# A decoder layer in split fp32 on one Trainium2 core: low weight parts of 30 column tiles through an adding DMA

## The chip, the cores and the metric

The kernel runs on one core of one Trainium2 chip. The metric is the device time of one execution in microseconds (us), the median of several runs.

## The reference: what is computed

One step of a hybrid decoder layer for a prompt of 512 tokens and 8 single sample tokens, width 1024, all in fp32. A normalised input goes through one combined projection `w_in` of 5632 columns. They feed three branches: A, a gated linear recurrence with a short convolution; B, a GLU with a causal depthwise convolution of 31 taps; C, a diagonal state space model with a GLU of its own. Three gates of 1024 columns each weigh the branches' projections; then come an output projection and a feed-forward block.

```
proj = rms_norm(x, g_mix) @ w_in
u_a, z_b, u_c, gate_in = split(proj)
y_a = rg_lru(causal_dwconv(u_a))
y_b = silu(layer_norm(causal_dwconv(z_b[:512] * sigmoid(z_b[512:]))))
y_c = glu(gelu(s5_ssm(u_c)))
g_a, g_b, g_c = sigmoid(gate_in + b_gate)
x = x + (g_a * (y_a @ w_pa) + g_b * (y_b @ w_pb) + g_c * (y_c @ w_pc)) @ w_out
x = x + (silu(h2 @ w1) * (h2 @ w2)) @ w_ffn_out        where h2 = rms_norm(x, g_ffn)
```

## The kernel before

Activations lie transposed, channels on the 128 partitions and the 520 tokens along the free axis, in two halves of 260. A weight matrix is worked on in column tiles of 128 columns; for `w_in` each has 8 tiles of 128 rows.

**Split products.** TensorE takes its operands in a rounded form (type fp32r), so that each fp32 operand is split into a rounded high part and the rest, the low part. `prod` (L243 to 251) does for each column tile high times high, high times the activations' low part, and then low weights times high activations: 48 matmuls of 260 columns in two halves, the 32 with the high weights ahead of the 16 with the low ones.

**Weights.** `wload` (L214) loads a pair of column tiles (1 MB) into `wraw`, by a DMA on the queue of SyncE (SP); there are two such buffers, so that a load waits until both columns of the pair before the last have been read. `wsplit` (L222) makes the parts of one column: ScalarE writes the high part `whi` (L225), and DVE or GpSimd (POOL), whichever `eng` names, subtracts it from the raw column and writes the low part `wlo` (L226). `whi` and `wlo` have three buffers each, so the parts of column n go where those of column n-3 lay. `wcol` (L231) calls both, with high priority.

```
whi, wlo: bufs=3        wraw: bufs=2
S.activation(hi, raw, AF.Copy)
e.tensor_tensor(lo, raw, hi.bitcast(F32), op=ALU.subtract)
```

The keys of `w_in`'s column tiles are `w.in.0` to `w.in.43`: branch A's 0 to 7, B's 8 to 15, C's 16 to 19, and the gates 20 to 43.

**Order.** PE's order of work is written out by hand (the string `ORDER`). The instructions of the other engines are put in an order when the kernel is built, by a scheduler with priorities; each engine and each DMA queue then works in that order. SP's queue carries, beside the raw weights, the loads `h<-ud_d` for branch C (`c_prep`, L870), the gate weights `w_rg` and `w_ig` of branch A (`a_load`, L1082), and the stores of finished gates, `g_d<-t` (`gate`, L1296). On DVE the 116 instructions of the 31 taps (`b_conv`, L1231) have low priority and fill in. An activation is split by ScalarE (L257) and DVE or GpSimd (L258).

**Names at the places of the prediction.** On GpSimd `pend_s` (L932), the copy of `s_rho` (L817), `fin_a` (L1134, L1135) and L938 to L941 are small steps of the states of branches A and C. `t L257` is the high part of a product of a gate or of branch A.

Of the kernel before, what the change touches and what calls it, by code (L numbers as in the profile page):

```python
# [16 lines left out]
F32 = mybir.dt.float32  # L17
F32R = mybir.dt.float32r
I32 = mybir.dt.int32
AF = mybir.ActivationFunctionType  # L20
ALU = mybir.AluOpType
# [10 lines left out]
ON_POOL = set("""  # L32
ac.3 caz.2 caz.3 ebz.0 ebz.1 ebz.2 ebz.3 hs.0 hs.2 hs.4 hs.5 rho.1 rho.2 rho.3 w.glu.3 w.in.0 w.in.10 w.in.11 w.in.2
w.in.3 w.in.36 w.in.38 w.in.39 w.in.4 w.in.8 w.w_out.3 w.w_pa.2 w.w_pa.5 w.w_pa.6 w.w_pb.1 w.w_pb.4 w.w_pb.5 w.w_pc.2
w.w_pc.3 wrg.6 ya.5 yg.0 yg.2
""".split())

ON_DVE = set("""
ca.0 ca.1 ca.2 ca.3 wt.0 wt.1 wt.2 wt.3
""".split())  # L40
# [15 lines left out]
def hybrid_step(ctx: ExitStack, tc, a, o):  # L56
    nc = tc.nc
    V, S, G, T, Y = nc.vector, nc.scalar, nc.gpsimd, nc.tensor, nc.sync
# [10 lines left out]

    def eng(key):  # L70

        return G if key in ON_POOL else V

    uid = [0]

    def nm(s):
        uid[0] += 1
        return f"{s}_{uid[0]}"
# [4 lines left out]
    def ht(shape, dt=F32):  # L83
        return hp.tile(shape, dt, tag="h", name=nm("h"))
# [70 lines left out]
    def vload(names, eng):  # L155
        nonlocal at
        for name in names:
            src = a[name][0]
            src = (src.rearrange("k (t p) -> (k t) p", p=P) if name.startswith("w_conv") else
                   src.rearrange("(t p) -> t p", p=P))  # L160
            VB[name] = at
            eng.dma_start(vrow[at:at + src.shape[0], 1, :], src)
            at += src.shape[0]
# [58 lines left out]
    def wsplit(raw, nk, e, dst=None):  # L222
        hi, lo = dst or (wp.tile([P, nk, P], F32R, tag="whi", name=nm("whi"), bufs=3),
                         wp.tile([P, nk, P], F32R, tag="wlo", name=nm("wlo"), bufs=3))
        S.activation(hi, raw, AF.Copy)  # L225
        e.tensor_tensor(lo, raw, hi.bitcast(F32), op=ALU.subtract)  # L226
        return hi, lo

    pend = {}
# [1 line left out]
    def wcol(src, key, c, nk, k0=0, pair=True, dst=None):  # L231

        with tc.high_priority():
            e = eng(f"w.{key}.{c}")
            if not pair:
                return wsplit(wload(src, c * P, nk, P, k0), nk, e, dst)
            if (key, c) not in pend:
                raw = wload(src, c * P, nk, 2 * P, k0)
                pend[(key, c)] = raw[:, :, 0:P]
                pend[(key, c + 1)] = raw[:, :, P:2 * P]  # L240
            return wsplit(pend.pop((key, c)), nk, e)
# [203 lines left out]
    for k in range(8):  # L445
# [8 lines left out]
                           op=ALU.mult))  # L454
# [307 lines left out]
    def c_pool(ct):  # L762

        d = st_c.setdefault(ct, {})
        E = eng(f"eb.{ct}")
        s_ = slice(4 * ct, 4 * ct + 4)
        eb = d["eb"] = ht([P, 2, 4, P])
# [28 lines left out]

        E = V if f"wt.{ct}" in ON_DVE else G
        wt = d["wt"] = ht([P, 2, 4, P])
# [21 lines left out]
    def c_pool2(ct):  # L820

        d = st_c[ct]
        s_ = slice(4 * ct, 4 * ct + 4)
        E = V if f"ca.{ct}" in ON_DVE else G
        ca = d["ca"] = ht([P, 2, 4, P])
# [534 lines left out]
    for c in range(8):  # L1360
        w = wcol(a["w_out"][0], "w_out", c, 8)
# [4 lines left out]
        hi, lo = fh[c // 4][:, c % 4, :], fl[c // 4][:, c % 4, :]  # L1366
# [135 lines left out]
    for half, (f0, f1) in enumerate(((0, 12), (12, 22))):  # L1502
        act = {}
        for f in range(f0, f1, 2):
# [9 lines left out]
            for j in range(2):  # L1514
                w = wcol(w_fi, "fi", f + j, 8)
# [11 lines left out]
            for j in range(2):  # L1527
                w = wcol(w_fi, "fi", NF + f + j, 8)
# [24 lines left out]
        for c in range(8 if half == 0 else 4):  # L1553
            w = [wcol(w_fo, "fo", c, hk, k0=f0 + j * hk, pair=False) for j in range(2)]
# [11 lines left out]
    for h in range(2):  # L1566
        for c in range(4, 8):
            ps = mm()
            for j in range(2):
# [9 lines left out]
                hi, lo = wk[c, j]  # L1579
# [54 lines left out]
```

## Time and profile before

| | |
|---|---|
| median of 3 runs | 908.58 us (907.57 to 910.23) |
| the profiled execution | 913.02 us |
| its span in the trace | 910.4 us |
| mean granted clock of TensorE | 0.978 |
| PE busy | 859.9 us |
| DVE busy | 584.2 us |
| ScalarE (ACT) busy | 359.5 us |
| GpSimd (POOL) busy | 211.5 us |

The durations below come from the one profiled execution, which took 913.02 us; the span is the part of it that the trace covers. PE are the matmuls; the trace gives for each instruction its start, its duration and the idle time ahead of it with what ended that.

### The profile page before, as it was taken

What the parts mean: (1) busy time and instruction counts of PE and PEld (TensorE: products, weight loads), DVE (VectorE), ACT (ScalarE), POOL (GpSimd) and SP (SyncE); (2) the same over time, 40 slices, a digit from 0 to 9 for tenths busy, and PEclk for the clock granted to TensorE, in tenths of its full rate; (3) what the DMA queues carried; (4) which work ended last, traced back from release to release, by engine and by line L of the source; (5) the groups of instructions that cost most, each with busy time, mean ns of one, the idle gap of its engine ahead of it and who ended that gap; (6) DMA issues with size and microseconds to landing.
All of it is one profiled execution on the core that took longest, in us unless ns stands there. A gap on an engine that the chain in (4) does not pass through costs nothing.

```text
span 910.4 us, 17515 instructions
## 1 busy us (share of the span) xinstructions
PE 859.9 (94%) x7329; PEld 849.6 (93%) x7329; DVE 584.2 (64%) x977; ACT 359.5 (39%) x553; POOL 211.5 (23%) x294
## 2 busy tenths in 40 slices
PE   6989999879978499999999999999999999999997
PEld 5989999779878499999999999999999999999997
DVE  6799969777899999986674454444432344443443
ACT  5543243546467564516343433333211232233321
POOL 6467474426332602214111200000000000000021
PEclk9989999999998599999999999999999999999999
DMA  5833224232321126554262223332233432311322
GB/s 190 260 128 105 84 93 128 61 94 71 116 70 60 58 94 188 196 175 166 70 233 93 93 93 121 96 98 67 70 87 90 155 94 93 117 62 46 101 73 94
DMA packets 103630, 99.73 MB, mean 110 GB/s; under 512 B 8676, under 2 KB 94936, under 8 KB 103024
## 3 DMA queue, kind: packets, MB, share of 16 engines
q1 hardware_dynamic: 103215, 98.01, 33.8%
q8 instruction: 57, 0.93, 0.4%
q0 software_dynamic: 320, 0.57, 0.2%
q14 instruction: 22, 0.17, 0.1%
q10 hardware_dynamic: 16, 0.03, 0.0%
HBM read 86.57 MB, written 12.58 MB: 109 GB/s over the span
## 4 chain that ended last, share of the span: by engine, by line
PE 75%; DVE 12%; DMA 3%; POOL 3%; ACT 3%; issue 2%; SPq 1%; DVEq 0%; POOLq 0%; ACTq 0%
PE mm L251 69%; PE mm L1583 3%; DVE t L1231 3%; DMA t<-w_ig 1%; DVE wlo L226 1%; DVE q L1231 1%; SPq L198 1%; DMA wraw<-w_in 1%; ACT t L137 1%; DMA q<-x_prompt 1%; DMA g_d<-t 1%; POOL t L938 1%; POOL fin_a L1134 1%; DVE t L418 1%; ACT whi L225 0%
## 5 line engine op out<-in xcount | busy, mean ns | idle before, releaser
L251 PE MATMUL mm<-q,whi 128*128 128x260 f32 x3296 | 418.8, 284 | 1.4 <-ACT q L257 0.6
L251 PEld LDWEIGHTS mm<-q,whi 128*128 128x128 f32 x3296 | 405.4, 189 | 3.2 <-ACT t L137 1.0
L226 DVE TENSOR_TENSOR wlo<-wraw,whi 128x1024 fp32r<-128x1024 f32 (+3 forms) x126 | 140.2, 1113 | 219.3 <-PE mm L251 122.6
L225 ACT ACTIVATE whi<-wraw 128x1024 fp32r<-128x1024 f32 (+3 forms) x146 | 139.1, 956 | 239.3 <-PE mm L251 220.2
L251 PE MATMUL mm<-q,wlo 128*128 128x260 f32 x1648 | 215.4, 282 | 0.0
L251 PEld LDWEIGHTS mm<-q,wlo 128*128 128x128 f32 x1648 | 204.5, 188 | 0.0
L251 PE MATMUL mm<-h,whi 128*128 128x260 f32 x800 | 106.4, 287 | 2.9 <-DVE h L258 2.9
L251 PEld LDWEIGHTS mm<-h,whi 128*128 128x128 f32 x800 | 101.5, 192 | 3.5 <-DVE h L258 3.4
L1455 POOL TENSOR_TENSOR t<-t,t 128x260 f32<-128x260 f32 (+1 forms) x9 | 8.4, 931 | 370.9 <-DVE h L1430 336.5
L226 POOL TENSOR_TENSOR wlo<-wraw,whi 128x1024 fp32r<-128x1024 f32 (+1 forms) x20 | 43.4, 2168 | 76.1 <-PE mm L251 53.4
L251 PE MATMUL mm<-h,wlo 128*128 128x260 f32 x400 | 56.2, 286 | 0.0
L1231 DVE SCALAR_TENSOR_TENSOR t<-q,vec,t 128x512 f32<-128x512 f32 x71 | 53.3, 778 | 0.0
L251 PEld LDWEIGHTS mm<-h,wlo 128*128 128x128 f32 x400 | 52.2, 192 | 0.0
L137 ACT ACTIVATE t<-mm,vec 128x520 f32<-128x520 f32 x44 | 30.1, 693 | 37.9 <-PE mm L251 16.2
L137 ACT ACTIVATE t<-t,zero_t 128x520 f32<-128x520 f32 x30 | 21.5, 729 | 56.6 <-DVE t L1524 56.6
L251 PE MATMUL mm<-t,t 128*128 128x260 f32 x96 | 19.1, 361 | 23.9 <-ACT t L257 19.5
L251 PEld LDWEIGHTS mm<-t,t 128*128 128x128 f32 x96 | 16.7, 254 | 25.8 <-ACT t L257 20.4
L131 ACT ACT_TABLE_LOAD x22 | 28.2, 1283 | 1.1 <-PEq L1622 0.7
L257 ACT ACTIVATE h<-t 128x520 fp32r<-128x520 f32 x18 | 11.5, 637 | 42.7 <-DVE t L591 42.7
L1231 DVE SCALAR_TENSOR_TENSOR q<-q,vec 128x512 f32<-128x512 f32 x30 | 27.7, 923 | 0.4
L1120 POOL TENSOR_TENSOR t<-t,t 128x520 f32<-128x520 f32 x8 | 12.4, 1556 | 40.9 <-DVE t L1231 22.7
L591 DVE TENSOR_TENSOR t<-t,t 128x520 f32<-128x520 f32 x30 | 20.8, 700 | 0.7
(401 smaller groups left out, 913.1 us busy)
## 6 DMA issues: line engine op xcount, KB each, us to landing
wraw<-w_ffn_in SPq DMA_DIRECT2D x22, 1024.0 KB
wraw<-w_in SPq DMA_DIRECT2D x20, 1024.0 KB
g_d<-t SPq DMA_DIRECT2D x24, 260.0 KB
t<-g_d SPq DMA_DIRECT2D x24, 260.0 KB
wraw<-w_ffn_out SPq DMA_DIRECT2D x16, 384.0 KB
wraw<-w_ffn_out SPq DMA_DIRECT2D x16, 320.0 KB
wraw<-w_pa SPq DMA_DIRECT2D x4, 1024.0 KB
wraw<-w_out SPq DMA_DIRECT2D x4, 1024.0 KB
```

The costliest lines, as they stand in the source:

```text
L131: last_tab[0] = after(S.preload_act_table_set(SETS[func]), last_tab[0])
L137: last_tab[0] = after(S.activation(out, x, func, **kw), last_tab[0])
L198: Y.dma_start(craw[:, ri, hf, q * 64:(q + 1) * 64], a[n][0].rearrange("(h s q) c p -> h q s c p", h=2, q=2)[hf, q])
L225: S.activation(hi, raw, AF.Copy)
L226: e.tensor_tensor(lo, raw, hi.bitcast(F32), op=ALU.subtract)
L251: T.matmul(ps[:, h, 0:HN], w_, x[:, h * HN:(h + 1) * HN], start=first and i == 0, stop=last and i == n - 1)
L257: S.activation(hi, src, AF.Copy)
L418: seq("v", V.scalar_tensor_tensor(out, x, gmx[:, k:k + 1], r, op0=ALU.mult, op1=ALU.mult))
L591: V.tensor_tensor(out, x, y, op=ALU.mult)
L1120: G.tensor_tensor(ig, ig, c, op=ALU.mult)
L1231: ins = V.scalar_tensor_tensor(x, win(k), wdw(k, t), x, op0=ALU.mult, op1=ALU.add)
L1583: T.matmul(ps[:, 0, 0:HN], w[:, k, :], x[:, h * HN:(h + 1) * HN], start=j == 0 and k == 0 and i == 0, stop=j == 1 and k == hk - 1 and i == 2)
```

## The change

For 30 of the 44 column tiles of `w_in` (`ON_DMA`: branch A's, all of the gates but 36 and 37) the low part is made in another way. ScalarE writes the high part as before, then writes the negated rounded column into `wlo`, and a DMA on GpSimd's queue adds the raw column to what lies there. The source of that DMA is one half of the pair: 1,024 runs of 512 bytes. Without the change 24 of the 30 subtractions are DVE's and 6 GpSimd's.

```diff
--- before.py
+++ after.py
@@ -33,6 +33,12 @@
 ac.3 caz.2 caz.3 ebz.0 ebz.1 ebz.2 ebz.3 hs.0 hs.2 hs.4 hs.5 rho.1 rho.2 rho.3 w.glu.3 w.in.0 w.in.10 w.in.11 w.in.2
 w.in.3 w.in.36 w.in.38 w.in.39 w.in.4 w.in.8 w.w_out.3 w.w_pa.2 w.w_pa.5 w.w_pa.6 w.w_pb.1 w.w_pb.4 w.w_pb.5 w.w_pc.2
 w.w_pc.3 wrg.6 ya.5 yg.0 yg.2
+""".split())
+
+ON_DMA = set("""
+w.in.0 w.in.1 w.in.2 w.in.3 w.in.4 w.in.5 w.in.6 w.in.7 w.in.20 w.in.21
+w.in.22 w.in.23 w.in.24 w.in.25 w.in.26 w.in.27 w.in.28 w.in.29 w.in.30 w.in.31
+w.in.32 w.in.33 w.in.34 w.in.35 w.in.38 w.in.39 w.in.40 w.in.41 w.in.42 w.in.43
 """.split())
 
 ON_DVE = set("""
@@ -69,7 +75,7 @@
 
     def eng(key):
 
-        return G if key in ON_POOL else V
+        return None if key in ON_DMA else G if key in ON_POOL else V
 
     uid = [0]
 
@@ -223,7 +229,12 @@
         hi, lo = dst or (wp.tile([P, nk, P], F32R, tag="whi", name=nm("whi"), bufs=3),
                          wp.tile([P, nk, P], F32R, tag="wlo", name=nm("wlo"), bufs=3))
         S.activation(hi, raw, AF.Copy)
-        e.tensor_tensor(lo, raw, hi.bitcast(F32), op=ALU.subtract)
+        if e is None:
+
+            S.activation(lo, raw, AF.Copy, scale=-1.0)
+            G.dma_start(lo.bitcast(F32), raw, accum_op=ALU.add)
+        else:
+            e.tensor_tensor(lo, raw, hi.bitcast(F32), op=ALU.subtract)
         return hi, lo
 
     pend = {}
```

Line numbers behind `wsplit` are higher by 11 after the change. The scheduler also orders the engines anew; three places matter to the prediction.

**SP, the second load of a raw pair behind place A** (`wraw` a pair of columns, `h_2703` and `h_2713` the same tile of branch C, `t_2687` and `t_2697` the gate weights). Before:

```order
L218 DMA wraw_3183<-w_in 128x8x256
L870 DMA h_2703<-ud_d 32x4x136
L870 DMA h_2703<-ud_d 32x4x128 x2
L1082 DMA t_2687<-w_rg 128x2x128
L1082 DMA t_2687<-w_ig 128x2x128
```

After:

```order
L224 DMA wraw_3197<-w_in 128x8x256
L1093 DMA t_2697<-w_rg 128x2x128
L1093 DMA t_2697<-w_ig 128x2x128
L1307 DMA g_d<-t_2631 128x520
L881 DMA h_2713<-ud_d 32x4x136
L881 DMA h_2713<-ud_d 32x4x128
L1307 DMA g_d<-t_2688 128x520
```

The loads of `w_rg` and `w_ig` and a store of a gate have passed the loads from `ud_d`.

**GpSimd ahead of place A** (`wlo` rows are the adding DMAs; `wraw_2575` is the pair whose release lets the next load on SP start). Before:

```order
L932 COPY pend_s<-h_1827 128x4 x2
L881 MEMSET t_2269 128x96
L827 MEMSET h_2301 128x1024
L1071 COPY fin_a<-q_804 128x3
L1072 COPY fin_a<-q_804 128x8
```

After:

```order
L943 COPY pend_s<-h_1829 128x4 x2
L235 DMA wlo_2475<-wraw_2209 128x8x128
L892 MEMSET t_2276 128x96
L235 DMA wlo_2578<-wraw_2575 128x8x128
L838 MEMSET h_2308 128x1024
L235 DMA wlo_2635<-wraw_2575 128x8x128
L1082 COPY fin_a<-q_804 128x3
L1083 COPY fin_a<-q_804 128x8
```

Three adding DMAs stand between the same small steps.

**DVE at place D** (L1119 to L1133 before, L1130 to L1144 after: branch A's recurrence; L1231 and L1242: taps of the convolution, L1245 its last sum). Before:

```order
L591 TENSOR_TENSOR t_3439<-t_3439,t_2796 128x520
L1231 SCALAR_TENSOR_TENSOR t_3144<-q_801,vec,t_3144 128x2x256
L591 TENSOR_TENSOR t_3441<-t_3441,t_3142 128x520
L226 TENSOR_TENSOR wlo_3862<-wraw_3802,whi_3861 128x1024
L1231 SCALAR_TENSOR_TENSOR t_3149<-q_801,vec,t_3149 128x2x256
L1130 SCALAR_TENSOR_TENSOR q_803<-t_2787,t_3439 128x256
```

After:

```order
L1245 TENSOR_TENSOR t_3158<-t_3158,t_3163 128x2x256
L1138 TENSOR_TENSOR t_3481<-t_3147,h_806 128x8
L1130 SCALAR_TENSOR_TENSOR t_3457<-t_2797,t_3457 128x520
L1130 SCALAR_TENSOR_TENSOR t_3459<-t_3147,t_3459 128x520
L602 TENSOR_TENSOR t_3457<-t_3457,t_2806 128x520
L602 TENSOR_TENSOR t_3459<-t_3459,t_3156 128x520
L1141 SCALAR_TENSOR_TENSOR q_803<-t_2797,t_3457 128x256
L1139 TENSOR_TENSOR t_3481<-t_3481,t_3459 128x8
L1141 SCALAR_TENSOR_TENSOR q_803<-t_3147,t_3459 128x256
L1142 SCALAR_TENSOR_TENSOR q_803<-t_2797,q_803,t_3457 128x256
L1144 COPY q_803<-t_3481 128x2x4
L1142 SCALAR_TENSOR_TENSOR q_803<-t_3147,q_803,t_3459 128x256
```

The taps and the subtraction that stood between the recurrence's steps are gone from there; the taps stand ahead.

## Rows read from the trace of the kernel before

**Rows 1.** The page, busy time of each engine (share of the span) and instructions.
```profile
PE 859.9 (94%) x7329; PEld 849.6 (93%) x7329; DVE 584.2 (64%) x977; ACT 359.5 (39%) x553; POOL 211.5 (23%) x294
```

**Rows 2.** By stretch: busy us (count) of each engine, granted clock, DMA share, GB/s.
```profile
250.00:275.00 25.00, 19.33 (x156) 19.12 (x155) 25.00 (x39) 14.80 (x18) 7.62 (x6) 0.95 0.24 79
300.00:325.00 25.00, 16.79 (x94) 15.97 (x95) 25.00 (x33) 12.22 (x19) 14.32 (x12) 0.66 0.22 71
350.00:900.00 550.00, 549.11 (x4568) 547.83 (x4567) 278.57 (x366) 183.64 (x241) 45.00 (x34) 1.00 0.34 107
```

**Rows 3.** TensorE's waits: for what, us in total, times, longest us.
```profile
PE mm L251 <- ACT t L257: 19.5, 4, 9.1
```

**Rows 4.** Instructions on the raw weights: count, then ns min/median/max.
```profile
L226 DVE TENSOR_TENSOR wlo<-wraw,whi x126: 670/1222/2333, 30.4 to 878.7; 128x1024 fp32r<-128x1024 f32 x86, 128x768 fp32r<-128x768 f32 x16, 128x512 fp32r<-128x512 f32 x14, 128x640 fp32r<-128x640 f32 x10
```

**Rows 5.** Timeline of PE, two columns: start us, us, instruction [idle before].
```profile
326.74 4.02 PE L251 MATMUL mm<-q,whi 128*128 128x260 f32 x32
332.51 4.01 PE L251 MATMUL mm<-q,whi 128*128 128x260 f32 x32
```

**Rows 6.** GpSimd's DMA issues (timeline), their landings (transfers), the hardware queue.
```profile
33.01 0.63 POOL L184 DMA_DIRECT2D t<-w_dw_b  x1
33.65 0.52 POOL L185 DMA_DIRECT2D t<-b_dw_b  x1
...
t<-state_cfm_conv POOLq DMA_DIRECT2D x2, 240.0 KB, 3.6
t<-w_dw_b POOLq DMA_DIRECT2D x1, 62.0 KB, 2.5
...
q1 hardware_dynamic: 103215, 98.01, 33.8%
```

**Rows 7.** Timelines at place A, of ScalarE, DVE, SP and PE.
```profile
162.12 1.05 ACT L225 ACTIVATE whi<-wraw 128x1024 fp32r<-128x1024 f32 x1
163.21 1.23 DVE L226 TENSOR_TENSOR wlo<-wraw,whi 128x1024 fp32r<-128x1024 f32 x1 [1.19 <-ACT whi L225]
164.46 0.37 SPq L218 DMA_DIRECT2D wraw<-w_in  x1
164.88 2.00 SPq L870 DMA_DIRECT2D h<-ud_d  x4
171.51 2.09 PE L903 MATMUL mm<-h,h 128*128 128x136 f32 x16 [1.88 <-DMA h<-ud_d]
```

**Rows 8.** Timelines at place B, of GpSimd, DVE, SP and ScalarE.
```profile
188.26 0.75 POOL L817 COPY t<-s_rho 128x512 f32<-128x512 f32 x1
190.22 1.22 DVE L226 TENSOR_TENSOR wlo<-wraw,whi 128x1024 fp32r<-128x1024 f32 x1
191.94 1.54 SPq L870 DMA_DIRECT2D h<-ud_d  x3
199.73 0.63 ACT L257 ACTIVATE t<-t 128x512 fp32r<-128x512 f32 x1 [3.22 <-DMA t<-w_ig]
```

**Rows 9.** Timelines at place C, of GpSimd and ScalarE.
```profile
215.96 0.64 POOL L1134 COPY fin_a<-q 128x1 f32<-128x1 f32 x1 [1.84 <-DVE q L1133]
217.28 4.33 POOL L1134 COPY fin_a<-q 128x1 f32<-128x1 f32 x1
230.58 0.69 ACT L137 ACTIVATE t<-mm,vec 128x520 f32<-128x520 f32 x1 [8.14 <-POOL t L940]
```

**Rows 10.** Timelines at place D, of DVE and PE.
```profile
232.25 1.23 DVE L226 TENSOR_TENSOR wlo<-wraw,whi 128x1024 fp32r<-128x1024 f32 x1 [2.14 <-ACT whi L225]
268.88 1.22 DVE L226 TENSOR_TENSOR wlo<-wraw,whi 128x1024 fp32r<-128x1024 f32 x1
270.02 0.75 DVE L1231 SCALAR_TENSOR_TENSOR t<-q,vec,t 128x512 f32<-128x512 f32 x1
270.68 0.69 DVE L1130 TENSOR_TENSOR_SCAN q<-t,t 128x256 f32<-128x256 f32 x1
273.30 1.02 PE L251 MATMUL mm<-t,t 128*128 128x260 f32 x3 [5.67 <-ACT t L257]
```

## The prediction

> **What bounds the kernel now.** I read the page's first line, then the table by stretch, then TensorE's waits, and last the timelines of the places where those waits end. The first shows PE busy for 94% of the span [rows 1]: almost all the time is matmuls, which this change doesn't touch. The table says where the rest lies. From 350 us to 900 PE is busy 549.11 of 550 us; between 250 and 325 it isn't (19.33 of 25 us, and at the end 16.79 at a granted clock of 0.66), and there DVE is busy all 25 us [rows 2]. So whatever the change does for DVE, it can only win something before 325 us, and there the reader must look at who is waited for. The costliest wait is PE on ScalarE's split t L257: 19.5 us in four places [rows 3]. Each of the four hangs on a different chain, so I went through them one by one: A (171 us), B (200 us), C (217 to 231 us), D and E (273 and 302 us).
>
> **What leaves and what comes.** Thirty column tiles lose their subtraction: 24 of 1.2 us on DVE (median 1222 ns [rows 4]; the next instruction starts some 1.13 us after it [rows 10]) and 6 on GpSimd. Each gains a second ScalarE activation like the one that writes the high part (1.05 us [rows 7], I use 1.06), and one adding DMA of 512 KB on GpSimd's queue. ScalarE pays 30 x 1.06 = 32 us; its busy share is 39% [rows 1], and after 350 us PE hides it, so there I count nothing. The cover is the ring of three: the low part of column n goes where that of column n-3 lay, and is needed two columns of 5.77 us plus one high part of 4.02 us later [rows 5], some 15.5 us. ScalarE's 1.06 and the DMA fit into it if the DMA lands within about 14 us. If that cover failed, PE would stand once per column.
>
> **What an adding DMA costs** the trace of before doesn't show, so I bound it. Issue on GpSimd: 0.52 us for a tiny load and 0.63 us for one of 124 runs [rows 6]. The new one has 1,024 runs of 512 bytes; the slope of those two rows gives 0.52 + 0.11 x 1024/120 = 1.46 us. The ends are 0.52 (no slope) and 5.2 (all of the 0.63 grows with the runs); I take 1.46. Issue to landing, L: at least 3.6 us, the row of 240 KB. For the upper end: the 103,215 packets of the hardware queue took 33.8% of 16 engines' 910.4 us, 47.7 ns each; 1,024 of them on 16 engines are 3.05 us, beside the 2.5 us in which the 62 KB load landed [rows 6]: 5.6 us if the data passes once, 8.6 if the sum needs source and destination read one after the other. I take the middle of 3.6 and 8.6, L = 6.1, as the two packet sums lie on either side of it.
>
> The Trainium skill (DMA: Bandwidth & Descriptors, section Anatomy of one DMA — SWDGE (gpsimd) path) gives about 2.0 us and 436 GB/s for such a transfer, that is 3.2 us here, an estimate; nothing in this trace moves data from SBUF to SBUF, so no run here shows it. By it the sum below would be -1.0 us instead of +4.8, no change.
>
> **Place A, the release of the raw pair: +5.9.** The pair of raw columns has two buffers, and the load of the next pair waits on SP until the last subtraction has read the old one. Before: ScalarE's high part ends at 163.17, DVE's subtraction at 164.44, SP issues wraw at 164.46, and right behind it the four h<-ud_d loads, for which PE waits at 171.51 [rows 7]. SP is in order, and the order of SP is the same here after the change. Now the old pair is released when the negated part (1.06 behind the high part, 164.2) and then the DMA are through: 164.2 + L against 164.4, so A = L - 0.2 = +5.9, with ends +3.4 and +8.4. PE goes on where it waited already, so all of it is on the path.
>
> **Place B: +1.1.** The second DMA of its pair stands on GpSimd behind the two pend_s copies and that of s_rho, which ends at 189.0 [rows 8]; pend_s hangs on DVE, which loses one subtraction ahead, so 187.9. The release is then 187.9 + L against 191.44 (the subtraction at 190.22). But the w_rg and w_ig loads, for whose landing ScalarE's split at 199.73 waits, now pass three of the ud_d loads, which took 1.54 us on SP [rows 8]. B = L - 3.5 - 1.5 = L - 5.0 = +1.1, ends -1.4 and +3.6. Place 0, the pair before A, has the same shape, but none of PE's long waits hangs on it: I count nothing, with B's 3.6 as the high end.
>
> **Place C: +1.2.** GpSimd's chain of small copies ends ScalarE's wait of 8.14 us at 230.58, and two adding DMAs now stand in it: 2 x 1.46 = 2.9. Against it, three subtractions leave DVE there (3 x 1.13 = 3.4), and GpSimd's copies are slow just beside DVE's two-operand work (one form took 0.64 us, then 4.33) [rows 9]. Ends -0.5 and +2.9, the middle is +1.2.
>
> **Places D and E: -3.4.** From 232.25, where DVE last stood idle for 2 us, to E it works through a list. Six subtractions leave that list, the first at 232.25 and the last at 268.88, -6.8 us; five more taps of the convolution, which were interleaved behind it, now stand ahead of the last split, +5 x 0.67 [rows 10]. That is -3.4 net; PE's waits there are 5.7 and 9.1 us, wide enough to give it. Ends 0 (ScalarE's own table loads set E, whatever DVE does) and -6.8 (the taps fill gaps). What is late next there is the GpSimd chain of fin_a and the split itself.
>
> **Sum:** 5.9 + 1.1 + 1.2 - 3.4 = +4.8 us. Against the profiled execution (913.02 us, span 910.4) that is 917.8; this execution stands 4.4 above the median of the runs, 908.58, so the forecast is **913.4 us**. A difference under 0.3% (2.7 us) can't be told from no change in this kernel.
>
> **Rivals.** *Faster: the landing is short and DVE's relief is whole.* With L = 3.6, D and E -6.8 and C -0.5 the sum is 3.4 - 1.4 - 0.5 - 6.8 = -5.3, **903.3 us**. It decides at L = 6.3 where relief is whole (2L - 5.2 - 0.5 - 6.8 = 0), at L = 3.7 where it is only -3.4. For it: DVE is full from 250 on; against it: 1,024 runs of 512 bytes, and the rows of 124 runs land in 2.5 already.
>
> *Much slower: GpSimd can't issue while DVE works.* The row of 4.33 against 0.64 [rows 9] is a GpSimd instruction held 3.7 us beside DVE's work; if issuing is held so, A, B and C (twice) get 3.7 each, **928 us**. Against it: the issues of 0.52 and 0.63 [rows 6] were not held, though DVE ran only short instructions then. The Trainium skill (SBUF — State Buffer, section SBUF: two separate sides) has this as a trap: GpSimd cannot write descriptors while DVE holds the shared ports, in modes that a plain fp32 copy takes. The trace shows the hold for a copy on GpSimd, not for an issue.
>
> *Nothing measurable.* L near 4 and D and E -3.4 cancel out: 2L - 5.2 + 1.2 - 3.4 = +0.6, **909 us**. That the change doesn't do what it says, a DMA that lands too late for the ring of three, belongs to the much slower case: one column late costs its wait 30 times.
>
> **Chances.** The forecast 0.43, with its own range 911.4 to 920 (upper ends at A, B and C with -3.4 at D and E are +11.5); faster 0.30; much slower 0.10; nothing 0.17. So faster 0.30, same 0.17, slower 0.43 + 0.10 = 0.53. The range reaches from 901 (the faster rival, with 2.3 us for subtractions that leave DVE before 150 us) to 926 (all upper ends, 8.4 + 3.6 + 3.6 + 2.9 with D and E at 0, give 927); some 0.08 lies above and as much below.
>
> **What would show it.** Right: the wraw load at A issued near 170 us, with PE's wait for h<-ud_d near 7.8 instead of 1.9; L between 5 and 8 in the list of transfers; PE's wait for t L257 at D and E shorter by 3.4 together; PE full after 330 us. Wrong: an adding DMA that lands in 4 us; GpSimd issues of over 3 us beside busy DVE; a wait of PE for wlo after 330 us; or place A no longer hanging on SP.

## The result, and the profile after

The changed kernel takes 948.92 us (median of 4 runs, 944.5 to 951.42) where the kernel before takes 908.78: a ratio of 1.0437, 95% interval 1.0413 to 1.0461, 40 us more. The forecast was 913.4 with a range to 926. The profiled execution took 944.50 us; it stands 31.5 above the profiled one of before (913.02 us), which lay 4.2 above its median, while this one lies 4.4 below its own; so the traces explain 32 of the 40 us.

The page of the changed kernel: the busy time of each engine, and two DMA queues with packets, MB and share of 16 engines' time:

```profile
PE 871.1 (92%) x7329; PEld 859.8 (91%) x7329; DVE 550.9 (58%) x953; ACT 388.0 (41%) x583; POOL 229.3 (24%) x318
...
q1 hardware_dynamic: 103215, 98.01, 32.5%
q0 software_dynamic: 31520, 16.30, 15.1%
```

DVE has lost 33 us of work against [rows 1]. GpSimd has 18 more: 47 us of issuing, part of which overlaps its next instruction, less six subtractions. q1 moves the same packets as before [rows 6]; q0, which had 320 packets, has 31,520: (31,520 - 320)/30 = 1,040 for each adding DMA.

What one of them costs stands in the view of the tile wlo (GpSimd's issue: ns min/median/max; then from issue to landing):

```profile
L235 POOL DMA_DIRECT2D wlo<-wraw x30: 1537/1554/1912, 106.1 to 437.0; - x30
...
DMA to landing us min/median/max: 6.4/7.0/12.2
```

Both prices of the prediction were about right in the median: issue 1.55 us (1.46 forecast), L, the time from issue to landing, 7.0 (6.1, ends 3.6 and 8.6); the longest landing, 12.2 us, lies above the upper end. So it is not the median price that failed. The table by stretch (columns as in [rows 2]) shows where PE stands now:

```profile
200.00:225.00 25.00, 15.48 (x181) 14.37 (x180) 5.78 (x10) 12.08 (x19) 5.89 (x9) 0.80 0.65 128
350.00:375.00 25.00, 21.84 (x160) 21.42 (x159) 20.27 (x31) 10.56 (x17) 4.65 (x3) 0.86 0.66 150
```

New holes lie at 200 to 225 us, and behind 350, where PE had hardly waited before. TensorE's waits:

```profile
PE mm L262 <- ACT t L268: 22.4, 4, 7.9
...
PE mm L262 <- ACT t L143: 5.8, 3, 2.6
```

The wait for t L268 (L257 before) is no shorter than in [rows 3], the one for h<-ud_d grew from 1.9 us to 6.8 (place A below), and PE now waits for a low part itself (4.4 us, at 401.84 below), and for evictions (t L143: ScalarE moves a finished product out of `mm`).

PE's order is the same in both kernels, so the start of the same instruction in both gives the lag at that place (us):

| place | before | after | lag | gained there | forecast |
|---|---|---|---|---|---|
| 0 | 160.82 | 164.80 | 3.98 | +4.0 (0.4 of it before 130 us) | 0 |
| A | 171.51 | 180.37 | 8.86 | +4.9 | +5.9 |
| B | 200.41 | 218.12 | 17.71 | +8.9 | +1.1 |
| C | 232.86 | 251.43 | 18.57 | +0.9 | +1.2 |
| D and E | 311.71 | 331.18 | 19.47 | +0.9 | -3.4 |
| to the end of the span | 910.4 | 942.4 | 32.0 | +12.5 | 0 |

Place A went nearly as forecast. Timelines of ScalarE, GpSimd, SP and PE there:

```profile
165.61 1.04 ACT L234 ACTIVATE wlo<-wraw 128x1024 fp32r<-128x1024 f32 x1
...
167.00 1.55 POOL L235 DMA_DIRECT2D wlo<-wraw  x1 [7.08 <-ACT wlo L234]
...
173.80 0.37 SPq L224 DMA_DIRECT2D wraw<-w_in  x1
174.22 1.99 SPq L881 DMA_DIRECT2D h<-ud_d  x4
...
180.37 3.97 PE L914 MATMUL mm<-h,h 128*128 128x136 f32 x16 [6.80 <-DMA h<-ud_d]
```

The negation ends at 166.7, GpSimd issues at 167.00, and SP may load the next pair at 173.80, 6.8 us later; the h<-ud_d loads stand right behind, and PE waits for them ([rows 7] shows the same chain 9 us earlier and without the DMA). The wait costs a second time. PE had stood for 6.80 us, and then its granted clock was 0.50, the level of 1.2 GHz; the same 16 matmuls took 3.97 us where they took 2.09 in [rows 7]. Table by stretch, the 5 us behind the wait:

```profile
180.00:185.00 5.00, 4.63 (x21) 4.67 (x22) 0.69 (x1) 1.25 (x2) 1.35 (x4) 0.50 0.00 0
```

Place B is where the forecast was furthest off ahead of 331 us. SP before:

```profile
191.50 0.39 SPq L218 DMA_DIRECT2D wraw<-w_in  x1
...
194.01 0.47 SPq L1082 DMA_DIRECT2D t<-w_ig  x1
```

GpSimd, ScalarE, SP and PE after:

```profile
192.17 1.55 POOL L235 DMA_DIRECT2D wlo<-wraw  x1 [6.34 <-ACT wlo L234]
193.09 3.27 POOL L1082 COPY fin_a<-q 128x3 f32<-128x3 f32 x1
...
196.43 0.95 POOL L780 MEMSET h<- 128x1024 f32 x1
...
194.60 1.06 ACT L231 ACTIVATE whi<-wraw 128x1024 fp32r<-128x1024 f32 x1 [2.22 <-PE mm L262]
197.42 0.81 ACT L784 ACTIVATE h<-t 64x64 f32<-64x64 f32 x4 [1.75 <-POOL h L780]
198.25 1.06 ACT L234 ACTIVATE wlo<-wraw 128x1024 fp32r<-128x1024 f32 x1
...
199.67 1.55 POOL L235 DMA_DIRECT2D wlo<-wraw  x1 [0.68 <-ACT wlo L234]
...
206.20 0.39 SPq L224 DMA_DIRECT2D wraw<-w_in  x1
...
207.26 0.52 SPq L1093 DMA_DIRECT2D t<-w_ig  x1
...
217.44 0.63 ACT L268 ACTIVATE t<-t 128x512 fp32r<-128x512 f32 x1 [9.80 <-DMA t<-w_ig]
...
218.12 1.23 PE L262 MATMUL mm<-t,t 128*128 128x260 f32 x4 [6.62 <-ACT t L268]
```

The high part of the pair's second column is there at 195.7. ScalarE's next instruction is L784, which needs a memset of GpSimd (L780, 196.43); that stands on GpSimd behind the first adding DMA (192.17) and a copy that took 3.27 us. So the negation comes at 198.25 in place of 195.7, the DMA is issued at 199.67, and the pair is free at 206.20. Behind it on SP stand w_rg and w_ig; for w_ig ScalarE waits 9.80 us, and PE for ScalarE 6.62. ScalarE's split follows the issue of w_ig by 10.2 us (207.26 to 217.44), before by 5.7 (194.01 to 199.73): another 4.5 us. The adding DMA that took 12.2 us to land was issued at 205.23, so the two loads shared the DMA engines with it; that this made them slower is not shown by a run of its own.

Place C came out near the forecast by another path. ScalarE there:

```profile
245.98 0.70 ACT L143 ACTIVATE t<-mm,vec 128x520 f32<-128x520 f32 x1 [3.22 <-POOL t L951]
248.79 1.06 ACT L231 ACTIVATE whi<-wraw 128x1024 fp32r<-128x1024 f32 x1 [2.12 <-DMA wraw<-w_in]
```

Its wait for GpSimd's chain fell from 8.14 us [rows 9] to 3.22. Then it waited 2.12 us for a weight load, with the eviction behind it for which PE waits 2.60 us at 251.43.

Places D and E, where DVE's relief was to show:

```profile
290.40 0.75 PE L262 MATMUL mm<-t,t 128*128 128x260 f32 x4 [4.18 <-ACT t L268]
295.62 4.70 PE L262 MATMUL mm<-t,t 128*128 128x260 f32 x20 [4.48 <-DVE t L269]
323.39 1.24 PE L262 MATMUL mm<-t,t 128*128 128x260 f32 x4 [7.88 <-ACT t L268]
```

PE's waits of 5.67 [rows 10] and 9.1 us [rows 3] became 4.18 + 4.48 and 7.88.

The last 12.5 us are lost where I had counted nothing. First, GpSimd, SP, ScalarE and PE at 344 to 368 us:

```profile
344.32 1.57 POOL L235 DMA_DIRECT2D wlo<-wraw  x1 [2.42 <-ACT wlo L234]
...
350.98 0.37 SPq L224 DMA_DIRECT2D wraw<-w_pc  x1
...
357.07 0.63 ACT L231 ACTIVATE whi<-wraw 128x512 fp32r<-128x512 f32 x1 [5.55 <-DMA wraw<-w_pc]
...
361.02 6.57 PE L262 MATMUL mm<-q,whi 128*128 128x260 f32 x32 [1.69 <-ACT t L143]
```

An adding DMA is issued at 344.32; the next load of a raw pair (w_pc) starts at 350.98 and lands so late that ScalarE stands 5.55 us for it. Behind that in ScalarE's order stand evictions, for which PE waits 1.47 us and then 1.69; after that its granted clock is 0.50 (361 to 365 us), and 32 matmuls take 6.57 us in place of 4.0.

Second, the low part at 401.84; the kernel before at the same column, then the changed one:

```profile
366.67 2.10 ACT L225 ACTIVATE whi<-wraw 128x1024 fp32r<-128x1024 f32 x3
368.49 1.22 DVE L226 TENSOR_TENSOR wlo<-wraw,whi 128x1024 fp32r<-128x1024 f32 x1
...
372.25 2.07 PE L251 MATMUL mm<-q,wlo 128*128 128x260 f32 x16
```

```profile
392.24 1.06 ACT L231 ACTIVATE whi<-wraw 128x1024 fp32r<-128x1024 f32 x1
393.21 1.04 ACT L234 ACTIVATE wlo<-wraw 128x1024 fp32r<-128x1024 f32 x1
...
394.85 1.56 POOL L235 DMA_DIRECT2D wlo<-wraw  x1 [17.97 <-ACT whi L231]
...
393.35 4.11 PE L262 MATMUL mm<-q,whi 128*128 128x260 f32 x32 [0.87 <-ACT whi L231]
401.84 3.84 PE L262 MATMUL mm<-q,wlo 128*128 128x260 f32 x16 [4.38 <-DMA wlo<-wraw]
```

ScalarE, which works off other activations ahead of it, writes the high part only when PE is about to use it. What is left for the low part is one high part of matmuls, 4.1 us: the subtraction of 1.22 us fitted into that, the negation and a DMA that lands 7.0 us after its issue do not, and PE stands 4.38 us.

### The profile page after: what moved, and what is told of

Read it like the earlier page. It is cut to its first block, busy times and chain, and to the rows that moved or that the text cites. A ratio compares the mean times of both kernels' runs of the same rounds, so it can differ in the third digit from the quotient of the medians.

```text
span 942.4 us, 17608 instructions
## 1 busy us (share of the span) xinstructions
PE 871.1 (92%) x7329; PEld 859.8 (91%) x7329; DVE 550.9 (58%) x953; ACT 388.0 (41%) x583; POOL 229.3 (24%) x318
## 3 DMA queue, kind: packets, MB, share of 16 engines
q0 software_dynamic: 31520, 16.30, 15.1%
## 4 chain that ended last, share of the span: by engine, by line
PE 62%; DVE 14%; DMA 11%; ACT 5%; issue 4%; POOL 2%; SPq 2%; DVEq 0%; ACTq 0%; POOLq 0%
PE mm L262 57%; DMA wlo<-wraw 4%; PE mm L1594 3%; DVE t L1242 3%; DMA t<-w_ig 2%; DMA g_d<-t 1%; DMA wraw<-w_in 1%; DVE q L1242 1%; ACT t L143 1%; DMA wraw<-w_pc 1%; SPq L204 1%; ACT wlo L234 1%; ACT whi L231 1%; DVE h L798 1%; DVE wlo L237 1%
## 5 line engine op out<-in xcount | busy, mean ns | idle before, releaser
L237 DVE TENSOR_TENSOR wlo<-wraw,whi 128x1024 fp32r<-128x1024 f32 (+3 forms) x102 | 110.6, 1084 | 217.8 <-PE mm L262 122.9
L235 POOL DMA_DIRECT2D wlo<-wraw x30 | 47.0, 1567 | 102.1 <-ACT wlo L234 77.5
L1242 DVE SCALAR_TENSOR_TENSOR t<-q,vec,t 128x512 f32<-128x512 f32 x71 | 56.7, 838 | 0.8 <-ACT t L1238 0.7
L262 PEld LDWEIGHTS mm<-t,t 128*128 128x128 f32 x96 | 17.4, 265 | 32.0 <-ACT t L268 23.4
L143 ACT ACTIVATE t<-t,zero_t 128x520 f32<-128x520 f32 x30 | 21.5, 729 | 56.6 <-DVE t L1535 56.6
L237 POOL TENSOR_TENSOR wlo<-wraw,whi 128x1024 fp32r<-128x1024 f32 (+1 forms) x14 | 27.7, 1977 | 67.3 <-PE mm L262 43.8
L234 ACT ACTIVATE wlo<-wraw 128x1024 fp32r<-128x1024 f32 x30 | 31.7, 1055 | 18.6 <-PE mm L262 18.6
L143 ACT ACTIVATE t<-mm,vec 128x520 f32<-128x520 f32 x44 | 29.6, 687 | 20.4 <-PE mm L262 11.2
L268 ACT ACTIVATE h<-t 128x520 fp32r<-128x520 f32 x18 | 11.5, 637 | 43.0 <-DVE t L602 43.0
L269 DVE TENSOR_TENSOR t<-t,t 128x520 fp32r<-128x520 f32 (+1 forms) x10 | 6.9, 694 | 32.5 <-ACT t L268 25.5
```

The costliest lines, as they stand in the source:

```text
L143: last_tab[0] = after(S.activation(out, x, func, **kw), last_tab[0])
L234: S.activation(lo, raw, AF.Copy, scale=-1.0)
L235: G.dma_start(lo.bitcast(F32), raw, accum_op=ALU.add)
L262: T.matmul(ps[:, h, 0:HN], w_, x[:, h * HN:(h + 1) * HN], start=first and i == 0, stop=last and i == n - 1)
L268: S.activation(hi, src, AF.Copy)
L1242: ins = V.scalar_tensor_tensor(x, win(k), wdw(k, t), x, op0=ALU.mult, op1=ALU.add)
```

## The experiments

My theory R after reading the trace: the raw pair, of which there are two buffers, is held until the adding DMA has landed, so each weight load starts 7 us and more too late, and with it what stands behind it on SP; DVE's time is worth little against that. The rivals: Q, the negation and the issues stand in ScalarE's and GpSimd's queues ahead of work that others wait for; D, the adding DMAs take the DMA engines' time from the loads. The ratio given with each of e1 to e12 is to the kernel before; the brackets hold its 95% interval.

**e1: the same adding DMA, fed from HBM.**

```diff
-            G.dma_start(lo.bitcast(F32), raw, accum_op=ALU.add)
+            G.dma_start(lo, add_src.rearrange("(k p) c -> p k c", p=P), accum_op=ALU.add)
```

`add_src` is the column of `w_in` in HBM; the low part is also named by its rounded type here.

> As the changed kernel, but the adding DMA takes the raw column from w_in in HBM instead of from the raw pair in SBUF, so that the pair is released by ScalarE's negation (the low part is the same; the same 30 issues, 30 negations and 30 landings stay). Theory R (the raw pair, held until the adding DMA has landed, delays the next weight load and what is queued behind it on SP): most of the 40 us goes, 908 to 920 us. Rival Q (the engines' queues: ScalarE's negation waits for PE and holds the evictions behind it, GpSimd's issue waits and holds its small copies): 940 to 950. Rival D (the adding DMAs take the DMA engines' time from the weight loads): 940 to 955, since the bytes are the same and HBM reads are added.

Measured: 913.55 us, ratio 1.005 (1.0028 to 1.0073). Of the 40 us 5 are left, though the low parts land later than in the changed kernel, and the queue takes nearly as much of the DMA engines (transfers: packets, MB, share; KB each, median us to landing):

```profile
q0 software_dynamic: 31520, 16.30, 14.1%
wlo<-w_in POOLq DMA_DIRECT2D x30, 512.0 KB, 8.1
```

TensorE's waits in e1, and PE at the column of 401.84 above:

```profile
PE mm L262 <- ACT t L268: 10.6, 2, 9.3
PE mm L262 <- DMA wlo<-w_in: 8.9, 5, 3.9
...
368.99 3.18 PE L262 MATMUL mm<-q,wlo 128*128 128x260 f32 x16 [3.92 <-DMA wlo<-w_in]
```

The wait for t L268 fell from 19.5 us [rows 3] to 10.6, two places of four, and the pair's release no longer holds up h<-ud_d (PE waits 2.2 us for it, before 1.9); 8.9 us are lost to low parts that come late, 6.6 of them behind 325 us. R stands for the loss as a whole; D falls as its cause, and Q carries at most these few us net (e1 gains ahead of 327 us and loses behind, see the table below e12). But the low part at 401.84 is nearly as late with the pair free (3.92 us in place of 4.38), so that wait is not the hold's.

**e2: the negation alone.** The raw column is added by the engine that subtracted before, no DMA.

```diff
+        S.activation(lo, raw, AF.Copy, scale=-1.0)
+        e.tensor_tensor(lo, raw, lo.bitcast(F32), op=ALU.add)
```

> As the changed kernel, but the raw column is added by DVE or GpSimd (the engine that subtracted it before), no DMA: it isolates the 30 added ScalarE activations and their waits. Theory R: 908 to 916. Rival Q: 925 to 945 if ScalarE's part of it carries the loss. Rival D: about 909.

Measured: 911.6 us, 1.0038 (1.0023 to 1.0053). ScalarE's 30 activations cost 3.5 us, not 20: Q's part of ScalarE falls as far as the activations alone go.

**e3 and e4: the change by halves** (only the set ON_DMA cut: 14 tiles used before 200 us, or the 16 of the gates A and B).

> Only branch A's columns and gate C's (14 tiles: 0 to 7 and 38 to 43) go through the adding DMA, all used before 200 us. Theory R: the lag that PE had at 200 us in the changed kernel, some +15 to +18 us, 923 to 930. Rival D: contention with loads grows with the number of DMAs, 14 of 30, +19, 927. Rival Q: the same +15 to +20.

> Only the gate columns 20 to 35 (16 tiles) go through the adding DMA. Theory R: the stretch after 200 us alone, where the lag grew from 18 to 32 us, +10 to +16, 919 to 925; with e3 the two losses add up to about the whole. If a relief of DVE exists at all, it shows here, where DVE was full: 900 to 908.

Measured: e3 924.44 us, 1.0174 (1.0145 to 1.0203); e4 931.54, 1.0265 (1.0229 to 1.0301). The losses, 16.3 and 23.4 us, add up to the whole. For e3 the three theories had forecast nearly the same, so it doesn't tell them apart. My number for e4 was too low: the late tiles cost more than the early ones, and no relief of DVE shows.

**e5: holding the pair and nothing else.**

```diff
+        if held:
+            e.memset(raw[:, 0, 0:1], 0.0)
+            G.dma_start(dr.tile([P, nk, P], F32, name=nm("hold")), raw)
```

These lines follow the subtraction, which is back in place; the new tile lies in HBM.

> The kernel before, subtractions and all, but behind each of the 30 low parts a plain DMA on GpSimd's queue copies the raw column (the column's first word per partition is set to 0 after the subtraction, so that the copy must follow it) to a spare place in HBM: the raw pair is held as in the changed kernel, with no negation and no low part that comes late. Theory R: holding alone gives half of the loss or more, 925 to 955. If the loss needed the negation or the late low part: under 915.

Measured: 913.08 us, 1.0061 (1.0041 to 1.008): a miss for R as I had put it. But the plain copy is another DMA than the adding one:

```profile
q0 software_dynamic: 4640, 16.30, 5.8%
...
hold<-wraw POOLq DMA_DIRECT2D x30, 512.0 KB, 4.2
```

(4,640 - 320)/30 = 144 packets instead of 1,040, landed in 4.2 us instead of 7.0. Either the loss needs the negation too, or 4 us of holding mostly fit into the slack. e9 and e10 tell these apart.

**e6 and e7: fed from HBM where it helps.** e1 with the 22 tiles that PE uses before 310 us, and with the six whose subtractions lay in DVE's full list.

> e1 with only the 22 tiles that PE uses before 310 us (0 to 7, 20 to 23, 26, 27, 32, 33, 38 to 43); the eight behind keep their subtraction. In e1 PE waited 8.9 us for wlo in five places, all behind 325 us. Theory R with DVE's relief: 903 to 908, that wait gone and the rest of e1 kept. If e1's gains before 310 us were those of its order alone: 908 to 914.

> As e1 with only the six tiles whose subtractions lay in the list that DVE works off without a pause from 232 us on (22, 23, 26, 27, 32, 33). My term for D and E, -3.4 us with ends 0 and -6.8, by itself: 902 to 909. No relief: 908 or more.

Measured: e6 902.46 us, 0.9939 (0.9914 to 0.9963), faster than both kernels; e7 904.44, 0.9971 (0.9943 to 0.9999). e7 is my term for D and E by itself: -3.4 forecast, -3.2 found by the medians, with an interval that nearly reaches no change. TensorE's waits in e6:

```profile
PE mm L260 <- ACT t L266: 10.7, 2, 9.2
...
PE mm L260 <- DMA wlo<-w_in: 1.6, 1, 1.6
```

The waits for late low parts fell from 8.9 us to 1.6 (two of e1's five, 2.4 us, lay before 325 us, so the text put down ahead of e6 was wrong in "all"), and two of the four long waits for the split are still gone. Against e1 the eight late tiles cost 11.1 us, with no pair held.

**e8: what stands behind the load on SP.**

```diff
-            Y.dma_start(u4[32 * k:32 * k + 32, :, lo:hi], ...)
+            S.dma_start(u4[32 * k:32 * k + 32, :, lo:hi], ...)
-            Y.dma_start(raw[:, i], a[n][0, ...])
+            S.dma_start(raw[:, i], a[n][0, ...])
```

> The changed kernel, but the loads h<-ud_d, w_rg and w_ig are issued on ScalarE's queue, so that they no longer stand behind the weight loads on SP. If the delay goes through what is queued behind the weight load (PE's waits for h<-ud_d and for the split behind w_ig, some 18 us of lag by 218 us): 925 to 935. If it goes through the weight load's own landing: 943 to 952.

Measured: 938.37 us, 1.0335 (1.0299 to 1.0371), between the two. PE still waits 6.6 us for h<-ud_d, now because these loads stand in ScalarE's order. So the run doesn't say how the loss divides between the weight load and what stands behind it.

**e9: holding as long as the change does,** with e5's edit and an adding DMA.

```diff
-            G.dma_start(dr.tile([P, nk, P], F32, name=nm("hold")), raw)
...
+            G.dma_start(spares[-1], raw, accum_op=ALU.add)
```

The cut lines make four spare regions in HBM, fill them from `w_in` and take them in turn.

> As e5, the kernel before with its subtractions, but the 30 copies to HBM are adding DMAs (into four spare regions in turn, filled once from w_in), so that the pair is held about as long as in the changed kernel, 7 us or more in place of e5's 4.2, and the DMA engines work as much; still no negation and no late low part. Theory R (the length of the hold sets the loss, little up to some slack and then one for one): 928 to 950. If the loss needs the negation and the late low part together with the hold: 912 to 920, as e5.

Measured: 939.55 us, 1.034 (1.0305 to 1.0376). The hold is that of the change (transfers):

```profile
hold<-wraw POOLq DMA_DIRECT2D x30, 512.0 KB, 6.8
```

and PE's waits show the same chain, but also a cost of the edit, the four filling DMAs that GpSimd issues at the very start:

```profile
PE mm L919 <- DMA h<-ud_d: 10.9, 1, 10.9
...
PE mm L384 <- POOL ident masks.py:199: 7.3, 1, 7.3
```

PE's instruction at 59.49 us before (L753, 3.9 us of waiting) starts at 66.00 in e9, 6.5 us later. So of the 31 us some 25 are the hold's, with subtractions on DVE, no negation and no low part that comes late. A hold of 4.2 us cost 5 us, then, and one of 6.8 some 25: R holds for the loss as a whole. Where the hold costs them is told below e12.

**e10 and e11: a shorter adding DMA, and its control.** The pair is laid out column by column.

```diff
-    raw = wp.tile([P, nk, ncol], F32, tag="wraw", name=nm("wraw"), bufs=2)
+    raw = wp.tile([P, 2, nk, P], F32, tag="wraw", name=nm("wraw"), bufs=2)
...
```

The cut lines load such a pair of `w_in` by two DMAs.

> The changed kernel with the raw pair laid out column by column (w_in's pairs loaded by two DMAs of 512 KB), so that the adding DMA reads 4 KB per partition in one piece, not 8 runs of 512 bytes. If the source's runs set the adding DMA's time (1,040 packets each; e5's plain copies were 144 and landed in 4.2 us): landing 4 to 5 us, and by theory R 915 to 930. If its packets stay at 512 bytes: landing 7, 943 to 955.

> Control for e10: the kernel before with the same layout and loads, no adding DMA. 905 to 912 (nothing in its places A to E hangs on the load's runs).

Measured: e11 910.47 us, 1.0008 (0.9987 to 1.0028), no change. e10 926.41, 1.0194 (1.0166 to 1.0222), 22 us less than the change:

```profile
q0 software_dynamic: 4640, 16.30, 9.8%
...
wlo<-wraw POOLq DMA_DIRECT2D x30, 512.0 KB, 5.6
```

144 packets again, landed in 5.6 us. The loss falls with the landing in the changed kernel itself. The issue and the DMA engines' share fell too (0.86 us for 1.55, 9.8% for 15.1%), but e1, which kept both, lost only 5 us.

**e12: e6's 22 tiles, fed from the raw pair.**

> The changed kernel with only e6's 22 tiles through the adding DMA, the source being the raw pair in SBUF as in the change: against e6 (902.5 us) only the release of the pair differs, against the changed kernel only the eight tiles that PE uses behind 310 us. Theory R, with the lag of 19 to 21 us that the changed kernel had at 310 us: 926 to 932; the rest of the 40 us is then the stretch behind it. If the eight late tiles cost nothing: 940 to 948.

Measured: 931.41 us, 1.0239 (1.0201 to 1.0277). Against e6 the source differs, and with it little else (e1's edit): 29 us for the release of the pair. Against the change the eight late tiles are worth 17.5 us, and with them left out PE has no hole at 350 to 400 us (columns as in [rows 2]):

```profile
350.00:400.00 50.00, 50.00 (x420) 50.00 (x419) 49.96 (x79) 26.46 (x37) 8.88 (x8) 1.00 0.49 161
```

Two instructions of PE, at 326.74 and 379.90 us in the kernel before (53.16 us apart), tell what the late stretch costs by itself:

| run | the late tiles | starts at | and at | lost between |
|---|---|---|---|---|
| changed kernel | pair held, negation, DMA | 344.47 | 412.15 | 14.5 |
| e1 | negation, DMA, pair not held | 317.00 | 378.28 | 8.1 |
| e9 | pair held, subtraction | 350.83 | 404.74 | 0.8 |
| e2 | negation, no DMA | 325.72 | 378.88 | 0.0 |
| e12 | as before the change | 346.40 | 399.56 | 0.0 |

Ahead of 326.74 us the loss is the hold's: e1 lags behind the kernel before by -9.7 us there, the change by 17.7, e12 by 19.7, and e9, less the 6.5 at its start, by 17.6. Behind it the hold alone costs 0.8 us. More than half of that stretch's loss is there with no pair held, and only where the low part comes through a DMA; the other 6.4 us appear only where hold and DMA-made low part meet.

## Why the prediction was wrong

**The prices held, the places didn't.** Issue and landing were forecast at 1.46 and 6.1 us and measured at 1.55 and 7.0. Place A (+5.9 forecast, +4.9 found) came by the mechanism that was described. Place C (+1.2, +0.9) was luck: GpSimd's chain, which I had made longer, ended ScalarE's wait sooner, and PE waited for an eviction behind a late weight load. The 27 us between the forecast sum and the traces are 4.0 at place 0, 7.8 at B, 4.3 at D and E and 12.5 behind 331 us, less 1.3 at A and C.

**The step that failed first: "after 350 us PE hides it, so there I count nothing. The cover is the ring of three".** I took the room of the low part from the ring: two columns and one high part, some 15.5 us. But the ring only says when the buffer is free; the low part starts when ScalarE has written the high part, and at the column of 401.84 that is when PE begins it. The room there is one high part, 4.1 us, and PE stood 4.38 us for a DMA that lands in 7.0: the sign "a wait of PE for wlo after 330 us" that I had named. The rows of before show it already (high parts from 366.67, PE's low part at 372.25). It needs no hold: e1 loses 8.1 us of the stretch's 14.5. What I had worked out at place A, that the raw pair is held as well, I didn't carry to this stretch either; there a late w_pc load holds ScalarE, and with it evictions, but by e9 a hold with no negation costs only 0.8 us there. Why the two together cost 6 us more than each by itself is not shown.

**Place B (+1.1) was mis-sized by taking the negation as immediate** behind the high part. The trace after shows two in-order queues waiting on each other: ScalarE for a memset of GpSimd, which stands behind the first adding DMA. The hold grew from 8.3 us (high part at 183.23, next load at 191.50) to 11.6 (194.60 to 206.20), 3.3 us. Of the other 5.6, 4.5 are the later landing of w_ig, and 2.5 the lower clock behind the wait at A, less 1.5 for the loads that were passed. Place 0, on which I said that no long wait hangs, has the shape of B: the adding DMA issued at 147.17 us let the next load start only at 157.11, 9.9 us later, so w_ig was issued 4.5 us later than before (158.15 for 153.63), and PE waited 3.76 us for the split behind it. That is the high end that I had given it, 3.6 us.

**The gain at D and E (-3.4) exists, but not under the hold.** e7 finds it (-3.2 us, at the edge of what can be told); in the changed kernel the same six tiles hold the pairs and +0.9 is left. e6 and e12, which differ in the release, show the same: from C to the end of E (232.86 to 311.71 us before) PE gains 4.1 us in e6 and loses 2.5 in e12. The sum by the faster rival took a relief of -6.8, which no run shows, and the chance of 0.30 that I gave it overlooked that relief and release belong to the same 30 tiles.

**The rival "much slower", 928 us, had the wrong mechanism.** GpSimd's issues were not held by DVE: all 30 took 1.54 to 1.91 us, though DVE was busy for 58% of the span and through the whole of most of them. The Trainium skill's trap of descriptors that can't be written (SBUF — State Buffer, section SBUF: two separate sides) did not show with the operations of this kernel.

**The clock added to it.** Behind the wait at A the granted clock was 0.50 for 5 us and PE's matmuls took twice their time; behind 361.02 us 32 of them took 6.57 us in place of 4.0. I had priced waits at their length alone.

## What to carry to other kernels

When a DMA takes over the last read of a staging buffer, its landing is added to the time that the buffer is held: check the ring of the source as well as that of the result, in every stretch where the ring turns. And take the room of the result from the moment at which its first step really runs, which the trace before shows, not from the number of buffers: here it was 4 us and not 15.5. Feed such a DMA from the place that the staging buffer was loaded from, if nothing forbids it; here that was worth 35 us, and with the eight late tiles left out it beats the kernel before by 0.6%. Price what stands behind the held load in the same queue, and a wait of TensorE also by the granted clock behind it.

## What was not expected of the hardware

The adding DMA took less time with fewer packets. With 1,040 packets per DMA the queue took 15.1% of 16 engines' 942.4 us, 4.7 us each (before's 0.2% taken off), and landed in 7.0; with 144 packets, from a contiguous source, 9.8% of 922.8, 3.0 us each, and landed in 5.6; the plain copy of e5 5.8% of 911.1, 1.7 us, and landed in 4.2. In all three some 2.5 us lie beyond the engines' time (7.0 - 4.7, 5.6 - 3.0, 4.2 - 1.7). So at the same number of packets adding took longer than copying (e5 copied to HBM, so that the place it writes to differs too), and strided packets cost 72 ns (4.7 us x 16/1,040) where I had taken 47.7. The Trainium skill (DMA: Bandwidth & Descriptors, section Anatomy of one DMA — SWDGE (gpsimd) path) gives some 2.0 us fixed, near the 2.5 found here, and 1.2 us for these bytes at its rate, an estimate, which the adding DMA exceeds 2.5 to 4 times.

The plain copy of the same strided column made 144 packets where the adding DMA made 1,040, and its issue on GpSimd took 0.85 us instead of 1.55.
